# A hybrid decoder block on one core: staggered operand addresses, unit-by-unit mixer pairs and a planned passage

## The chip, the cores and the metric

The kernel runs on one NeuronCore of a Trainium2 chip. The metric is device time in microseconds (us) for one execution; lower is better. The kernel before took 1016.34 us (median of three runs, 1015.45 to 1016.57). TensorE does the matmuls, VectorE (DVE), ScalarE (ACT) and GpSimd (POOL) work on tiles, and transfers are issued on the queues of SyncE (SP) and GpSimd.

## What is computed

One layer on 512 tokens of 1024 channels, in float32: three mixer branches with gates, an output projection, and a convolutional feed-forward part.

```python
h = rmsnorm(x); proj = h @ w_in                 # -> B, C, v | u, ug | q | three gates
y_a = (B * conv3(C * v)) @ w_a_out
y_b = silu(layernorm(conv31(u * sigmoid(ug)) + bias)) @ w_b_out
k, vm = split(rmsnorm(mem) @ w_kv)              # 256 memory tokens, 4 heads
y_c = softmax(q k / 16) vm @ w_att_out
x = x + (sum_i sigmoid(gate_i) * y_i) @ w_o
u = conv3(rmsnorm(x) @ w_up)                    # 2 * 2816 columns
x = x + (silu(u_gate) * u_up) @ w_down
out = rmsnorm(x)
```

## The kernel before

Each float32 operand is split into a high part (rounded to the type that TensorE takes in one pass) and a low part (the rest). A product is three matmuls: high weights by high data, high by low, low by high. A block of weights is a *unit*: 128 x 1024 numbers, loaded by SP into one of six `wf` buffers, copied to `whi` by ACT (L306) and subtracted to `wlo` by DVE (L307). Four pairs of `whi` and `wlo` exist (`UNIT_BUFS`). Splits are written into the program some units ahead of their use.

*Mixer.* Time runs over four heads of keys and values (`k`, `v`), four heads of queries (`q`, `s`, `pt`, `o`), then gated pairs of columns (`ug`, `u`), gates and outputs of three branches (`g`, `y`, `C`, `V`, `B`). Two units hold one pair of 128-wide output columns: unit 0 has the first four blocks of 128 input channels, unit 1 the other four. `next_col` and `project` do one column at a time from both units: 16 matmuls with `whi` (L343, L344), then 8 with `wlo` (L347). Both units are held until the second column is done. Work of other engines is written into the program between columns, by `tick`: jobs that were put `beside` a coming column, and steps of the long convolution.

*Output projection.* `rows_product` computes `row` tiles: four groups of 128 tokens, two halves of 512 columns (L352 to L354). In the second half all matmuls of a token group stand together (24 each), so that each group's sum, norm and transposes (`tr`) can begin before the next group is done.

*Quads.* The matrix w_up is multiplied in a scheme with seven products per block of 2 x 2, the forms 1 to 7, over eleven groups of columns (`QUADS`). A product of form f for group q is `multiply(q, f)`: 24 matmuls of 256 columns (L949). Its moving operand is one of seven pairs of tiles: `fb00`, `fb10` and `fb11` are transposed blocks of the normed rows, and `ft5`, `ft7`, `ft6` and `ft4` are sums of blocks, made in that order, each from the one before. Their fourteen tiles are of 4096 bytes per partition. The weights are sums too: transfers on the POOL queue add to a buffer (L1044) and DVE adds buffers (L1073). ACT and DVE split each unit (L1048, L1052), read the banks back and apply the convolution (L1119, eight steps a group).

*Planner.* From the quads to the end the order is made by `Jobs`: each job has an engine, a cost, the jobs that it follows, and a due time worked out backwards from PE's order; of the jobs that can start first, the one due first is written next. The program order on PE, ACT and DVE is then fixed. Before the planner starts, the passage is written by hand: rows, transposes, `multiply(0, 1)`, splits of the remaining units, transposes of group 2, `multiply(0, 2)`, transposes of group 3. The planner's order goes on with (1,1), (1,2), (0,5), (0,6), (1,5), (0,7), (0,3), (0,4).

*Down.* Seven products with w_down in the same manner (`row` tiles again), then the last norm.

*Addresses.* Pools on the left side of SBUF follow one another after the small constants, pools on the right side hang from the other end. A tile of [128, 1], `mean_col`, stands among the constants on the left. In what follows, the *offset* of a matmul is the address of its moving operand less that of the next matmul's weights, whose load runs beside it, modulo 512 bytes. Offsets by the placement: 256 for the products with `h_hi` and `h_lo`, for keys and values, for all fourteen tiles of the quads and for down (where the units move and `zh`, `zl` are the weights); 448 for `o`, `ya` and the low `yb` tiles as moving operands of `y`, 256 for the high `yb` tiles; 64 for the output projection (the units move, the `mg` tiles are the weights); 192 for the scores `s`; 320 for `o` (`pt` moves, `vh` and `vl` are the weights).

Of the kernel before, what the change touches and what calls it, by code (L numbers as in the profile page):

```python
# [55 lines left out]
LOAD_BUFS = 6  # L56
UNIT_BUFS = 4
# [92 lines left out]
def hybrid_block_kernel(  # L150
# [24 lines left out]
    psum = ctx.enter_context(tc.tile_pool(name="psum", bufs=8, space=bass.MemoryType.PSUM))  # L175

# [146 lines left out]
    pair = {"n": 0}  # L323

    def next_col():

        j = pair["n"] % 2
        pair["n"] += 1
        if j == 0:
            freed[0] = taken[0]  # L330
            taken[0] += 2
            split_to(freed[0] + 3)
            pair["units"] = split[freed[0] : taken[0]]
        else:
            split_to(freed[0] + 4)
        return pair["units"], j

    def project(ps, col, hi, lo):

        (u, j), at = col, slice(col[1] * P, (col[1] + 1) * P)  # L340
        for k in range(KC):
            w_hi = u[k // 4][0][:, k % 4, at]
            nc.tensor.matmul(ps, w_hi, hi(k), start=k == 0, stop=False)  # L343
            nc.tensor.matmul(ps, w_hi, lo(k), start=False, stop=False)  # L344
        for k in range(KC):
            w_lo = u[k // 4][1][:, k % 4, at]
            nc.tensor.matmul(ps, w_lo, hi(k), start=False, stop=k == KC - 1)  # L347
# [64 lines left out]
    mean_col = const.tile([P, 1], F32, tag="mean_col", name="mean_col")  # L412
# [10 lines left out]
    load_to(2)  # L423
    mem_cols = [a_tile("mem") for _ in range(KC // 2)]
    for i, t in enumerate(mem_cols):
        nc.sync.dma_start(
            out=t.rearrange("p (k n) -> p k n", k=2),
            in_=mem_t[i * 2 * P : (i + 1) * 2 * P, :].rearrange("(k p) n -> p k n", p=P),
        )
# [103 lines left out]
    def keep_keys(ps):  # L533
        t = a_tile("k")
        for c in range(2):
            at = (slice(None), slice(c * N_MEM, (c + 1) * N_MEM))
            nc.vector.tensor_tensor(t[at], ps[at], r_mem["row"][:, :N_MEM], op=ALU.mult)
        keys.append(split_tile(t, "k", rows, rows))
# [27 lines left out]
    for h in range(HEADS):  # L566
        ps = p_tile("k")
        for c in range(2):
            project(ps[:, c * N_MEM : (c + 1) * N_MEM], next_col(), m_hi, m_lo)
            if c == 1:  # L570
                beside(2 if h == 0 else 0, lambda ps=ps: keep_keys(ps))
            tick()
# [20 lines left out]
    def queries(h):  # L593
        q = []
        for c in range(2):
            ps = p_tile("q")
            project(ps, next_col(), *hp)
            hi, lo = a_tile("qh", F32R), a_tile("ql", F32R)
            nc.scalar.activation(hi, ps, AF.Copy, scale=Q_SCALE)
            nc.vector.scalar_tensor_tensor(  # L600
                lo, ps, Q_SCALE, hi.bitcast(F32), op0=ALU.mult, op1=ALU.subtract
            )
            q.append((hi, lo))
            if c == 1:
                beside(1, lambda: scores(h, q))
                beside(3, lambda: attend(h))
                beside(4, lambda: weigh(h))
            tick()
# [141 lines left out]
    def glu(m):  # L750
        sg = []
        for _ in range(2):
            ps = p_tile("ug")
            project(ps, next_col(), *hp)
            t = a_tile("sg")
            nc.scalar.activation(t, ps, AF.Sigmoid)
            sg.append(t)
            tick(5)
        for i in range(2):
            ps = p_tile("u")  # L760
            project(ps, next_col(), *hp)
            u = a_tile("u", pool=temp)
            nc.vector.tensor_tensor(u, ps, sg[i], op=ALU.mult)
            u_tiles[m + i] = u
            conv_b_start(m + i)
            tick(4)
# [3 lines left out]
    def short_conv(m):  # L770
        cs, ts = [], []
        for _ in range(2):
            ps = p_tile("C")
            project(ps, next_col(), *hp)
            t = a_tile("C")
            nc.scalar.copy(t, ps)
            cs.append(t)
            tick(5)
        for i in range(2):
            ps = p_tile("V")  # L780
            project(ps, next_col(), *hp)
            nc.vector.tensor_tensor(cs[i], ps, cs[i], op=ALU.mult)
            ts.append(conv3(cs[i], "conv_a_w", m + i, KC))
            tick(2)
        for i in range(2):
            ps = p_tile("B")
            project(ps, next_col(), *hp)
            nc.vector.tensor_tensor(ts[i], ps, ts[i], op=ALU.mult)
            ya.append(split_tile(ts[i], "ya", part, part))
            tick(3)  # L790
# [3 lines left out]
    def gates(b, m):  # L794
        ps = p_tile("g")
        project(ps, next_col(), *hp)
        t = a_tile("g")
        nc.scalar.activation(t, ps, AF.Sigmoid, bias=par("b_gate", b * KC + m))  # L798
        tick(5)
        return t  # L800

    def merge(m, parts, gate, first=False, last=False):
        ps = p_tile("y")
        project(ps, next_col(), lambda k: parts[k][0], lambda k: parts[k][1])
        nc.vector.tensor_tensor(gate, ps, gate, op=ALU.mult)  # L805
        if first:
            merged[m] = gate
        else:
            nc.vector.tensor_tensor(merged[m], merged[m], gate, op=ALU.add)
        if last:  # L810
            merged[m] = split_tile(merged[m], "mg", part, part)
        tick(3)
# [5 lines left out]
    for m in range(0, KC, 2):  # L818
        gate = [gates(2, m + i) for i in range(2)]
        for i in range(2):  # L820
            merge(m + i, o_parts, gate[i], True)
# [3 lines left out]
    for m in range(0, KC, 2):  # L825
        gate = [gates(0, m + i) for i in range(2)]
        for i in range(2):
            merge(m + i, ya, gate[i])
    gate = [gates(1, m) for m in range(KC)]
    assert not conv_todo and not side  # L830
    for m in range(KC):
        merge(m, yb, gate[m], last=True)
# [6 lines left out]
    h2 = h2_pool.__enter__()  # L839

# [4 lines left out]
    def rows_product(half, parts, rows, n_k, staggered, done):  # L845
# [17 lines left out]
        for t in range(NT):  # L863
# [8 lines left out]
            nc.vector.tensor_tensor(rows[t][half], rows[t][half], ps[t], op=ALU.add)  # L872
            if done is not None:
                done(t)
# [7 lines left out]
    def h2_tile(key):  # L882
        return [
            h2.tile([P, 4, HALF], F32R, tag=key + s, name=name("f" + key + s)) for s in "hl"
# [9 lines left out]
    def transpose_rows(xn, t):  # L894
        r, at = t // 2, slice((t % 2) * P, (t % 2 + 1) * P)
        for i in range(2):
            ps = p_tile("tr").rearrange("p (k n) -> p k n", k=4)
            for k in range(4):
                nc.tensor.transpose(ps[:, k, :], xn[i][:, k * P : (k + 1) * P], ident)
            form = h2_forms.get(f"b{i}{r}")  # L900
            if form is not None:
                nc.scalar.copy(form[0][:, :, at], ps)
                nc.vector.tensor_tensor(
                    form[1][:, :, at], ps, form[0][:, :, at].bitcast(F32), op=ALU.subtract
                )
            nc.scalar.copy(blocks[i, r][:, :, at], ps)

    rows_product(0, merged, x1, KC, 0, None)
    h2_n = {}

    def x1_norm(t):
        h2_n[t] = norm_rows(x1[t], g_ffn)
        for i in range(2):
            nc.sync.dma_start(out=x1_kept[t, :, i * 512 : (i + 1) * 512], in_=x1[t][i])
        if 0 < t < NT - 1:
            transpose_rows(h2_n.pop(t - 1), t - 1)

    rows_product(1, merged, x1, KC, KC, x1_norm)
# [35 lines left out]
    for n, f in enumerate(((0, 1), (0, 2), (1, 1))):  # L954
        w_units[f] = split[N_UP + n]
    multiply(0, 1)
    freed[0] = N_UP + 1
    split_to(len(units))
    w_units[1, 2] = split[N_UP + 3]
    transpose_rows(h2_n.pop(2), 2)  # L960
    multiply(0, 2)
    transpose_rows(h2_n.pop(3), 3)

    for p in (part_pool, rows_pool, temp_pool):
        p.__exit__(None, None, None)
    zs = ctx.enter_context(tc.tile_pool(name="zs", bufs=1, side="right", reuse_waits="tile"))
    temps_pool = tc.tile_pool(name="temps", bufs=1, side="right", reuse_waits="tile")
    temps = temps_pool.__enter__()

    jobs = Jobs([("pe", 0, 1), ("pe", 0, 2)], {"DMA": -15.0}, {"wf": LOAD_BUFS})  # L970
# [23 lines left out]

    BLOCK = {"t5": "t5", "t7": (0, 1), "t6": (0, 0), "t4": (1, 0)}
    job("t5", "DVE", dve(1024), sum_t5)
    job("t7", "DVE", dve(1024), sum_t7, ["t5"])
# [16 lines left out]
    order = [(1, 1), (1, 2), (0, 5), (0, 6), (1, 5), (0, 7), (0, 3), (0, 4)]  # L1014
    for q in range(1, QUADS):
        if q > 1:
# [8 lines left out]
    uses = [("pe", q, f) for q, f in order]  # L1025
# [38 lines left out]
    for q in range(QUADS):  # L1064
# [5 lines left out]
        if q > 1:  # L1070
            split_job(("pe", q, 1), (q, 1), src("u"), 4, 256, [("ld", q, "u")])
        split_job(("pe", q, 5), (q, 5), src("s"), 4, 256, [("s5", q)])
# [17 lines left out]
    z = zs.tile([P, 2, PAIRS, SEQ], F32, tag="z", name="z")  # L1090

    def temp2(s, n):
        return temps.tile([P, 2, SEQ], F32, tag=s, name=name(s), bufs=n)
# [31 lines left out]
    def gated(q):  # L1125
        nc.vector.tensor_tensor(z[:, :, q, :], c_t[q, 1], c_t[q, 0], op=ALU.mult)

    for q in range(QUADS):
        pe = lambda f, q=q: ("pe", q, f)
        job(("r1", q), "ACT", actv(512), lambda q=q: read1(q),  # L1130
            [pe(1)] + ([("taps", q - 2, 0)] if q > 1 else []))
# [27 lines left out]
    for q, f in order:  # L1159
        after = []  # L1160
        if (q, f) not in ((1, 1), (1, 2)):
            after.append(("wl", q, f))
        if OPERAND[f][0] == "t":
            after.append(("fl", OPERAND[f]))
# [273 lines left out]
```

## Time and profile before

| | us |
|---|---|
| median of three runs | 1016.34 |
| lowest, highest | 1015.45, 1016.57 |
| time of the profiled execution | 1016.17 |
| its span, first to last instruction | 1014.4 |

The page lists busy time by engine, the span in slices, the chain that ended last, and groups of instructions. "PE" is the matmul, "PEld" the weight load that runs beside it, "PEclk" the granted share of the TensorE clock. The duration of a matmul row includes its passage through the array, so rows overlap: what one matmul costs a stream is the distance from its start to the next start, called the *pitch* here. The page's chain of work merges neighbours, and then shows the pitch as length by count.

### The profile page before, as it was taken

What the parts mean: (1) busy time and instruction counts of PE and PEld (TensorE: products, weight loads), DVE (VectorE), ACT (ScalarE), POOL (GpSimd) and SP (SyncE); (2) the same over time, 40 slices, a digit from 0 to 9 for tenths busy, and PEclk for the clock granted to TensorE, in tenths of its full rate; (3) what the DMA queues carried; (4) which work ended last, traced back from release to release, by engine and by line L of the source; (5) the groups of instructions that cost most, each with busy time, mean ns of one, the idle gap of its engine ahead of it and who ended that gap; (6) DMA issues with size and microseconds to landing.
All of it is one profiled execution on the core that took longest, in us unless ns stands there. A gap on an engine that the chain in (4) does not pass through costs nothing.

```text
span 1014.4 us, 13621 instructions
## 1 busy us (share of the span) xinstructions
PE 986.4 (97%) x5424; PEld 859.1 (85%) x5424; DVE 783.8 (77%) x955; ACT 466.2 (46%) x634; POOL 107.2 (11%) x84
## 2 busy tenths in 40 slices
PE   6999999999999999999999999988999999999997
PEld 6988888888888888888887788878999999988876
DVE  4784548888877888888665365469999999999986
ACT  5554453232222232232255533266767666765556
POOL 3400000000000000000040000102122111101500
PEclk9999999999999999999999999999999999999999
DMA  9642222333323232333232624648887977879972
GB/s 322 191 141 83 63 63 83 91 96 104 99 89 104 83 104 85 103 104 104 88 100 93 197 83 125 163 128 166 188 186 174 201 176 164 179 247 309 270 130 83
DMA packets 122831, 141.10 MB, mean 139 GB/s; under 512 B 4880, under 2 KB 103824, under 8 KB 122768
## 3 DMA queue, kind: packets, MB, share of 16 engines
q1 hardware_dynamic: 100688, 114.28, 35.5%
q0 software_dynamic: 21936, 25.96, 16.0%
q8 instruction: 42, 0.69, 0.3%
q14 instruction: 21, 0.17, 0.1%
q10 hardware_dynamic: 144, 0.01, 0.0%
HBM read 136.03 MB, written 4.19 MB: 138 GB/s over the span
## 4 chain that ended last, share of the span: by engine, by line
PE 90%; DVE 4%; ACT 4%; issue 1%; DMA 1%; POOL 0%; SPq 0%; ACTq 0%; DVEq 0%; POOLq 0%
PE quad L949 20%; PE row L353 5%; PE row L352 5%; PE row L354 5%; PE y L347 4%; PE y L344 4%; PE y L343 4%; PE g L347 4%; PE g L343 4%; PE g L344 4%; PE q L343 1%; PE q L344 1%; PE C L344 1%; PE u L344 1%; PE u L343 1%; PE ug L344 1%
## 5 line engine op out<-in xcount | busy, mean ns | idle before, releaser
L307 DVE TENSOR_TENSOR wlo<-wf,whi 128x1024 fp32r<-128x1024 f32 x123 | 158.8, 1298 | 37.2 <-ACT whi L306 36.4
L680 DVE SCALAR_TENSOR_TENSOR acc<-u,pk,acc 128x511 f32<-128x511 f32 (+14 forms) x240 | 176.7, 738 | 6.1
L306 ACT CAST whi<-wf 128x1024 fp32r<-128x1024 f32 x124 | 128.1, 1045 | 49.4 <-PE y L344 29.4
L1048 ACT CAST whi<-wf 128x1024 fp32r<-128x1024 f32 (+1 forms) x91 | 94.0, 1035 | 59.3 <-PE quad L949 32.3
L1052 DVE TENSOR_TENSOR wlo<-wf,whi 128x1024 fp32r<-128x1024 f32 (+1 forms) x91 | 109.0, 1204 | 10.8 <-ACT whi L1048 10.5
L343 PE MATMUL g<-h_hi,whi 128*128 128x512 f32 x192 | 75.0, 391 | 1.6 <-ACT whi L306 1.6
L1044 POOL DMA_DIRECT2D wf<-in_w_up x33 | 42.5, 1289 | 316.5 <-DVE wlo L1052 126.8
L344 PE MATMUL g<-h_lo,whi 128*128 128x512 f32 x192 | 74.8, 390 | 0.0
L353 PE MATMUL row<-wlo,zh 128*128 128x512 f32 x154 | 60.3, 392 | 1.0 <-DVE wlo L1052 1.0
L352 PE MATMUL row<-whi,zh 128*128 128x512 f32 x154 | 60.1, 390 | 0.1
L354 PE MATMUL row<-whi,zl 128*128 128x512 f32 x154 | 59.9, 389 | 0.0
L798 ACT ACTIVATE g<-g,pk 128x512 f32<-128x512 f32 x24 | 16.5, 689 | 89.8 <-PE g L347 89.7
L347 PE MATMUL g<-h_hi,wlo 128*128 128x512 f32 x192 | 47.4, 389 | 0.0
L805 DVE TENSOR_TENSOR g<-y,g 128x512 f32<-128x512 f32 x24 | 16.6, 692 | 39.8 <-PE y L347 39.8
L343 PEld LDWEIGHTS g<-h_hi,whi 128*128 128x128 f32 x192 | 36.0, 188 | 10.0 <-ACT whi L306 2.4
L344 PEld LDWEIGHTS g<-h_lo,whi 128*128 128x128 f32 x192 | 36.0, 188 | 7.6
L347 PEld LDWEIGHTS g<-h_hi,wlo 128*128 128x128 f32 x192 | 36.0, 188 | 7.5
L688 POOL TENSOR_TENSOR tot<-tot,acc 128x512 f32<-128x512 f32 x6 | 10.6, 1767 | 256.2 <-DVE acc L680 179.4
L353 PEld LDWEIGHTS row<-wlo,zh 128*128 128x128 f32 x154 | 28.9, 188 | 7.8 <-DVE wlo L1052 2.1
L352 PEld LDWEIGHTS row<-whi,zh 128*128 128x128 f32 x154 | 28.9, 188 | 6.7 <-DVE x L1336 0.7
L354 PEld LDWEIGHTS row<-whi,zl 128*128 128x128 f32 x154 | 28.9, 188 | 6.0
L1119 DVE SCALAR_TENSOR_TENSOR c<-u,pk,c 128x511 f32<-128x511 f32 (+1 forms) x44 | 32.2, 747 | 0.6
(273 smaller groups left out, 2818.2 us busy)
## 6 DMA issues: line engine op xcount, KB each, us to landing
wf<-in_w_in SPq DMA_DIRECT2D x72, 512.0 KB, 3.5
wf<-in_w_up SPq DMA_DIRECT2D x46, 512.0 KB, 4.7
wf<-in_w_up POOLq DMA_DIRECT2D x33, 512.0 KB, 6.2
wf<-in_w_kv SPq DMA_DIRECT2D x16, 512.0 KB, 7.0
wf<-in_w_down SPq DMA_DIRECT2D x15, 512.0 KB, 5.8
wf<-in_w_att_out SPq DMA_DIRECT2D x8, 512.0 KB, 3.5
wf<-in_w_a_out SPq DMA_DIRECT2D x8, 512.0 KB, 3.5
wf<-in_w_b_out SPq DMA_DIRECT2D x8, 512.0 KB, 4.8
```

The costliest lines, as they stand in the source:

```text
L306: nc.scalar.copy(hi, src)
L307: engine.tensor_tensor(lo, src, hi.bitcast(F32), op=ALU.subtract)
L343: nc.tensor.matmul(ps, w_hi, hi(k), start=k == 0, stop=False)
L344: nc.tensor.matmul(ps, w_hi, lo(k), start=False, stop=False)
L347: nc.tensor.matmul(ps, w_lo, hi(k), start=False, stop=k == KC - 1)
L352: nc.tensor.matmul(ps, s_hi, w_hi, start=start, stop=False, skip_group_check=again)
L353: nc.tensor.matmul(ps, s_hi, w_lo, start=False, stop=False, skip_group_check=again)
L354: nc.tensor.matmul(ps, s_lo, w_hi, start=False, stop=stop, skip_group_check=again)
L680: nc.vector.scalar_tensor_tensor(acc[:, s:], u_tiles[m][:, : SEQ - s], par("conv_b_w", (K_B - 1 - s) * KC + m), acc[:, s:], op0=ALU.mult, ...
L949: nc.tensor.matmul(ps[:, c, :], w[:, k, at], a[:, k, :], start=first and n == 0, stop=k == 3 and n == 2, skip_group_check=again,)
L1048: nc.scalar.copy(w_units[key][0], src())
L1052: nc.vector.tensor_tensor(lo, src(), hi.bitcast(F32), op=ALU.subtract)
```

## The change

Four things are changed.

1. *Addresses.* `mean_col` moves to a pool `edge` of 224 bytes at the far right end, ahead of the other right-hand pools. A `shift` tile of 32 bytes stands first in the pool of the quads' operands, and each of the fourteen tiles is 32 bytes longer. By the placement, all products `y` and the output projection come to offset 256, as the rest of the mixer's projections; `s` and `o` come to offset 0. The quads' tiles stand at `fb00` 288 and 320 (high, low), `fb10` 352 and 384, `fb11` 416 and 448, `ft5` 480 and 0, `ft7` 32 and 64, `ft6` 96 and 128, `ft4` 160 and 192. Down stays at 256.
2. *Mixer pairs.* `project_pair` takes one unit after the other: per unit both columns, and per block high by high, high by low, low by high. A unit is given back after its own 24 matmuls. `tick` follows each unit, as it followed each column. Two PSUM tiles are open for a pair.
3. *Start.* The two halves of the memory operand that the first unit needs are loaded before the second unit.
4. *Passage.* The second half of the rows does the first unit for all four groups at once (24 matmuls) and then 18 per group. The last group's sum, norm and the transposes of groups 2 and 3, the split of unit (1,2) and the copies of the blocks become jobs of the planner. The order begins (0,1), transposes of group 2, (0,2), (1,1), transposes of group 3, (1,2), (2,1), (2,2), (0,5), and so on. The planner's cost of a quad product goes from 24 x 0.12 to 24 x 0.115.

The matmuls, splits, transfers and bytes are the same in number, except that the keys' sums are read from two tiles.

```diff
+    edge = ctx.enter_context(tc.tile_pool(name="edge", bufs=1, side="right"))
+    mean_col = edge.tile([P, 56], F32, tag="mean_col", name="mean_col")[:, :1]
...
-    def project(ps, col, hi, lo):
-        (u, j), at = col, slice(col[1] * P, (col[1] + 1) * P)
-        for k in range(KC):
-            w_hi = u[k // 4][0][:, k % 4, at]
-            nc.tensor.matmul(ps, w_hi, hi(k), start=k == 0, stop=False)
-            nc.tensor.matmul(ps, w_hi, lo(k), start=False, stop=False)
-        for k in range(KC):
-            w_lo = u[k // 4][1][:, k % 4, at]
-            nc.tensor.matmul(ps, w_lo, hi(k), start=False, stop=k == KC - 1)
+    def project_pair(ps, hi, lo, done, n_conv=0):
+        for g in range(2):
+            w_hi, w_lo = next_unit()
+            for j in range(2):
+                at = slice(j * P, (j + 1) * P)
+                for i in range(4):
+                    k = 4 * g + i
+                    first, last = k == 0, k == KC - 1
+                    nc.tensor.matmul(ps[j], w_hi[:, i, at], hi(k), start=first, stop=False)
+                    nc.tensor.matmul(ps[j], w_hi[:, i, at], lo(k), start=False, stop=False)
+                    nc.tensor.matmul(ps[j], w_lo[:, i, at], hi(k), start=False, stop=last)
+                if g == 1:
+                    done(j)
+            tick(n_conv)
...
-    load_to(2)
     mem_cols = [a_tile("mem") for _ in range(KC // 2)]
     for i, t in enumerate(mem_cols):
+        load_to(1 + i // 2)
...
+    h2.tile([P, SHIFT // 4], F32, tag="shift", name="shift")
...
     def h2_tile(key):
         return [
-            h2.tile([P, 4, HALF], F32R, tag=key + s, name=name("f" + key + s)) for s in "hl"
+            h2.tile([P, 4 * HALF + 8], F32R, tag=key + s, name=name("f" + key + s))[
+                :, : 4 * HALF
+            ].rearrange("p (k n) -> p k n", k=4)
+            for s in "hl"
         ]
...
-    rows_product(1, merged, x1, KC, KC, x1_norm)
+    rows_product(1, merged, x1, KC, KC - 2, x1_done)
...
-    multiply(0, 1)
-    freed[0] = N_UP + 1
-    split_to(len(units))
-    w_units[1, 2] = split[N_UP + 3]
-    transpose_rows(h2_n.pop(2), 2)
-    multiply(0, 2)
-    transpose_rows(h2_n.pop(3), 3)
...
+    t = NT - 1
+    job(("xs", t), "DVE", dve(512), lambda: x1_sum(t, last_row["ps"]), ["wo"])
+    job(("sq", t, 0), "ACT", 1.2, lambda: x1_square(t), [("xs", t)])
+    job(("xn", t), "DVE", 2.3, lambda: x1_scale(t), [("sq", t, 0)], 0.2)
...
-    order = [(1, 1), (1, 2), (0, 5), (0, 6), (1, 5), (0, 7), (0, 3), (0, 4)]
+    order = EARLY + [(2, 1), (2, 2), (0, 5), (0, 6), (1, 5), (0, 7), (0, 3), (0, 4)]
...
+        if (q, f) == (0, 2):
+            job(("tr", 2), "PE", 0.87, lambda: transpose_rows(2))
+        if (q, f) == (1, 2):
+            job(("tr", 3), "PE", 0.87, lambda: transpose_rows(3), [("xn", 3)])
-        job(("pe", q, f), "PE", 24 * 0.12, lambda q=q, f=f: multiply(q, f), after)
+        job(("pe", q, f), "PE", 24 * 0.115, lambda q=q, f=f: multiply(q, f), after)
```

## The prediction

> **What bounds the kernel now.** I read the page first, then busy times by stage, then the chain of waits merged by pitch, then what PE waited for.
>
> ```profile
> span 1014.4 us, 13621 instructions
> ...
> PE 986.4 (97%) x5424; PEld 859.1 (85%) x5424; DVE 783.8 (77%) x955; ACT 466.2 (46%) x634; POOL 107.2 (11%) x84
> ```
>
> PE is the bound, so time can come only from its idle stretches or from a shorter pitch. The busy times by stage (PE's first; after the engines PEclk and the DMA share) say where the 28 us of idle lie and who is next:
>
> ```profile
> 0.00:66.00 66.00, 54.74 (x405) 53.55 (x406) 46.38 (x59) 37.28 (x60) 19.98 (x19) 0.97 0.71 227
> ...
> 440.00:612.00 172.00, 170.41 (x743) 138.88 (x742) 109.87 (x132) 67.82 (x86) 14.68 (x9) 1.00 0.35 110
> 612.00:667.00 55.00, 55.00 (x248) 44.94 (x247) 26.84 (x38) 19.33 (x34) 2.73 (x2) 1.00 0.47 130
> 667.00:702.00 35.00, 28.64 (x219) 27.60 (x218) 29.05 (x31) 23.40 (x33) 6.41 (x5) 0.95 0.69 147
> 702.00:891.00 189.00, 189.00 (x1577) 189.00 (x1577) 177.46 (x198) 125.13 (x155) 33.40 (x26) 1.00 0.84 184
> 891.00:960.00 69.00, 68.33 (x337) 57.93 (x337) 65.62 (x67) 40.12 (x45) 18.65 (x16) 1.00 1.00 285
> ```
>
> The start idles 11.3 us, the passage (667 to 702) 6.4 us with the clock at 0.95. In the quads PE never stops, but DVE (third pair of numbers) is busy 177.5 of 189 us, 94%: it is the next bound. The merged chain gives pitches as length by count:
>
> ```profile
> 188.74 1.81 PE ug L347 x8
> ...
> 237.81 1.87 PE y L347 x8
> ...
> 701.25 190.10 PE quad L949 x1582
> ```
>
> That is 226.7 ns for 512 columns at offset 256, 233.3 at offset 448, and 120.0 for the quads' 256 columns at 256 (120.2 with the gaps of one wait). The half-clock stretches give what streaming alone costs: in 9.84 to 17.3 us the 256 columns of `k` start 213.3 ns apart, so 106.7 at full clock, and 213.3 for 512. Quads and `ug` both pay 13.3 ns over that, `y` pays 20. One stream of 256 columns has another offset, the scores at 192; here are two of its heads, start times in the first column:
>
> ```profile
> 83.56 0.28 PE L352 MATMUL s<-kh,qh 128*128 128x256 f32 x1
> ...
> 84.27 0.28 PE L352 MATMUL s<-kh,qh 128*128 128x256 f32 x1
> ```
> ```profile
> 98.14 0.28 PE L352 MATMUL s<-kh,qh 128*128 128x256 f32 x1
> ...
> 99.16 0.28 PE L352 MATMUL s<-kh,qh 128*128 128x256 f32 x1
> ```
>
> Six matmuls in 0.71 us are 118 ns each, nine in 1.02 us are 113: the same offset settles in two rhythms. The mean over all heads' starts is 114.6. So the pitch does go with where the operands lie. What PE waited for:
>
> ```profile
> PE k L343 <- ACT mh L452: 8.1, 1, 8.1
> PE quad L949 <- DVE ft5l L1007: 2.8, 1, 2.8
> PE g L343 <- ACT whi L306: 1.6, 2, 0.8
> PE quad L949 <- DVE wlo L1052: 1.4, 1, 1.4
> PE quad L949 <- ACT whi L306: 1.4, 1, 1.4
> ...
> PE quad L949 <- DVE wlo L307: 0.8, 1, 0.8
> ```
>
> **The change, part by part.** All sums stand against the profiled execution, 1016.2 us, of which 1014.4 is span; it lies 0.2 under the median of the runs.
>
> *Start: 3 us less.* Half a megabyte (the second unit) no longer goes ahead of the memory operand; at the page's 322 GB/s of the first slice that is 1.6 us. But the third matmul now wants `wlo` of the first unit, which POOL makes from 6.35 to 8.69 us, so PE starts in earnest near 8.5 instead of after its wait for the second `whi` until 11.84. From 8.5, 46 matmuls at 213 ns end near 18.3 (near 16.5 if full clock comes one step sooner); before, they end at 19.2: 0.9 to 2.7 less. Later, PE stands 2 us near 60 us behind a `whi` queued on ACT after `h_hi`, which waits for DVE's `x`; the half clock that follows costs about 1.4 more. Splits now run three units ahead instead of two, but DVE is nearly full from 46 to 70 us, so I take half of that back. Bounds: 0 (DVE eats it all) to 6.
>
> *Gates: 1.9 less.* The two waits of `g` at 554 and 566 us (starts 1.19 apart instead of 0.23) come from units queued on ACT behind the swish of four tiles, 5 us. A unit is now used for 5.4 us and three are ahead: covered. Without that cover the 1.9 us stay.
>
> *Offsets of `y` and of the output projection: 3.8 less.* At 256 like `ug`: 384 matmuls with `o` and `ya` by 6.6 ns are 2.5; 192 with `yb` (now 228.9) by 2.2 are 0.4; 192 of the projection (now about 231.5) by 4.8 are 0.9. Bounds: 0, since `yb` has a rhythm of 229 ns and more even where its offset is 256, and 3.8. `s` and `o` at offset 0 are 144 matmuls; between 113 and 126.7, and 226 and 233, they move 1.2 us at most: counted as nothing.
>
> *Passage: 6 less.* Lost now: 6.4 idle and 5% of 35 us, 1.8, at the lower clock, together 8.1. The chain in the new order, with durations from the rows: the split of (0,1) stands before the rows' norms, so the first quad's two waits (1.4 and 0.8) go. `ft5` needs both last transposes, one copy (0.6), a sum (1.2), ACT's cast (1.05) and DVE's low part (1.2), with three splits of DVE between; products (1,2), (2,1) and (2,2) stand ahead of it, 8.3 us: covered by about 1.5 us, and without it 2.8 and a new half-clock stretch of 1.6 return. What is late next: the first transposes, whose norm now has 4.1 us of matmuls over it instead of 5.6, but takes 4.9 with its table load (649.0 to 653.9): 0.8; and `wlo` of (0,3), last in a row of some seventeen DVE instructions of 1.2 us: about 1.4. So 8.1 less 2.2. The second half's SP writes wait for the sums as before, and the loads queued behind them have their buffers early. Bounds: 2 to 8.
>
> *Quads: 3.5 less.* No row shows thirteen of the fourteen offsets. Bounds by the nearest: 113.3 (a head of `s`) and 126.7 (the 20 ns that `y` pays at 448, put on 106.7). One of the fourteen, `ft4` low, is exactly the 192 of `s`. I take 117, midway between the scores' mean and the present value: 1848 matmuls by 3 are 5.5. Of this DVE takes back some: a quad costs it seven splits of 1.22, eight taps of 0.747, two sums of 0.68, one of 0.69 and two of 1.22, 19.0 us, against 168 x 0.117 = 19.7 of PE, and six instructions of 1.2 for down fall in besides. I charge 2 us. Ends for this term: 12.4 less to 12.4 more.
>
> "TensorE: Matmul & The Clock Gate" of the Trainium skill (Step-by-step) speaks against this part: PE has two independent read ports, and loading the next weights doesn't steal bandwidth from the running matmul. By that no offset would matter. The trace disagrees with 226.7, 233.3, 113 and 118.
>
> Sum: 3 + 1.9 + 3.8 + 6 + 3.5 = 18.2, so 998.
>
> **The rivals.**
>
> *The offsets do nothing* (chance 0.12): the differences of pitch come from rhythm alone, quads stay at 120. For it: one offset has two pitches. Against it: 1600 matmuls in one rhythm without a break. Then only start, gates and passage count, 10.9: 1005.
>
> *DVE becomes the bound* (0.18). From 667 to 960 us it has 272.2 us of work in 293. If it keeps idling 6%, as now in the quads, that stretch can't fall under 289.6. For it: the sums of the passage come in one run. Against it: much of its idling is waiting for `whi`, which waits for PE. Then the last two terms give 3.4 together: 1016.2 - 12.1 = 1004.
>
> *The quads get slower, 122 to 126.7* (0.12): offsets near 0 and 448 are as bad as `y` says; 3.7 to 12.4 lost against 14.7 won: 1005 to 1014.
>
> *The change loses* (0.08): an offset near 0 may cost more than any row shows. It decides from a mean of 120 + 14.7/1.848 = 128 ns on; at 132 it is 1016.2 - 14.7 + 22.2 = 1024.
>
> *Pitch near 113 and DVE keeps up* (0.10): 12.4 for the quads and 16.7 with the full passage: 987.
>
> **How the numbers follow.** The forecast has 0.40, with 993 to 1003 as its own range. From 988 to 1010 about 0.8 lies: the best case, the worst end of slower quads and the losing case are outside. A change of 0.2%, 2 us, is what a measurement here tells from none. Faster by more: all cases but the losing one and the worst end of slower quads, 0.89; within: 0.03; slower: 0.08.
>
> **What would show it.** Quads' matmuls of one form start at their own distance, between 113 and 127 ns, the same for all groups. `y` merges at 1.81 for eight. No wait of PE for `ft5l`; waits for `xn` near the first transposes and for `wlo` of (0,3). DVE over 96% in the quads. I am wrong if the quads' mean lies outside 114 to 121, or if PE waits for DVE more than 6 us between the rows and down.

## The result, and the profile after

The changed kernel takes 1005.84 us (median of four runs, 1003.44 to 1006.45) against 1016.46 for the kernel before (1015.45 to 1016.99): a ratio of 0.9892, 95% interval 0.9874 to 0.991. That is 10.6 us less: inside the range of 988 to 1010, but 7.8 short of the forecast of 998 and outside the 993 to 1003 that the forecast kept as its own. The profiled execution is the fastest of the four (1003.44, granted clock 0.997; the others 0.993 to 0.994), so its span is 12.8 us under that of the kernel before, more than the 10.6 between the medians. Its stages stand like this, in us, each from its first matmul to the next stage's (down is counted from the start of the quads' last matmul):

| | start, to first `q` | `q` to rows | rows | quads | down, to its last matmul |
|---|---|---|---|---|---|
| before | 66.75 | 554.28 | 47.92 | 231.67 | 106.84 |
| after | 62.97 | 549.18 | 45.80 | 223.24 | 113.15 |
| difference | -3.8 | -5.1 | -2.1 | -8.4 | +6.3 |

Four stages gave 19.4 us in this execution, a little more than the 18.2 forecast. Down, which the change doesn't touch, took 6.3 back. The page of the profile after:

```profile
span 1001.6 us, 13638 instructions
...
PE 975.7 (97%) x5424; PEld 853.4 (85%) x5424; DVE 784.7 (78%) x955; ACT 466.4 (47%) x632; POOL 106.5 (11%) x84
```

The busy times by stage (PE's first, DVE's third):

```profile
0.00:66.00 66.00, 55.85 (x420) 54.82 (x421) 48.66 (x59) 37.71 (x61) 20.73 (x19) 0.97 0.71 235
440.00:612.00 172.00, 172.00 (x761) 142.41 (x760) 112.76 (x137) 70.51 (x87) 13.73 (x9) 1.00 0.36 113
612.00:665.00 53.00, 52.94 (x271) 44.76 (x270) 26.82 (x40) 22.29 (x40) 1.44 (x1) 1.00 0.41 118
665.00:700.00 35.00, 33.60 (x283) 33.19 (x282) 33.08 (x34) 24.33 (x33) 10.29 (x8) 1.00 0.96 200
700.00:880.00 180.00, 179.32 (x1514) 178.90 (x1514) 165.22 (x187) 118.73 (x149) 30.84 (x24) 1.00 0.88 187
880.00:950.00 70.00, 63.24 (x279) 50.72 (x278) 67.92 (x69) 39.37 (x44) 20.79 (x18) 1.00 1.06 284
```

The idle time of the gates (440 to 612) is gone, that of the passage (665 to 700) falls from 6.4 to 1.4 at full clock. In the quads DVE is busy 92%, less than the 94% before, and yet in the first 70 us of down PE idles 6.8 us beside a DVE that is busy 97%. What PE waited for:

```profile
PE k L338 <- ACT mh L447: 6.5, 1, 6.5
PE row L348 <- ACT zh L1268: 2.8, 1, 2.8
PE row L348 <- DVE x L1403: 2.4, 2, 1.4
PE ss L469 <- POOL sq L437: 1.9, 1, 1.9
...
PE row L349 <- DVE wlo L1111: 1.3, 2, 0.9
PE quad L990 <- DVE wlo L1111: 1.3, 1, 1.3
```

The waits of `ft5l` and of the gates are gone. New are one for POOL's squares at the start and those of `row` in down. The longest of these, in PE's timeline:

```profile
892.01 0.39 PE L350 MATMUL row<-whi,zl 128*128 128x512 f32 x1
895.21 0.50 PE L348 MATMUL row<-whi,zh 128*128 128x512 f32 x1 [2.81 <-ACT zh L1268]
```

ACT casts that `zh` from the last product z (L1186), and DVE's timeline shows where the z was:

```profile
880.98 1.22 DVE L1186 TENSOR_TENSOR z<-c,c 128x1024 f32<-128x1024 f32 x1
...
884.38 2.98 DVE L1179 SCALAR_TENSOR_TENSOR c<-g,pk,c 128x511 f32<-128x511 f32 x4
...
888.41 2.98 DVE L1179 SCALAR_TENSOR_TENSOR c<-u,pk,c 128x511 f32<-128x511 f32 x4
891.49 1.23 DVE L1186 TENSOR_TENSOR z<-c,c 128x1024 f32<-128x1024 f32 x1
```

The quads' last matmul starts at 881.19. DVE still has the z of group 9 in hand and ends that of group 10 at 892.7, 11.5 us after the quads. Before, this lag was 7.9 us. So DVE came late out of a stage in which it had idled 8%.

### The profile page after: what moved, and what is told of

The parts are those of the page before. It is cut to its first block, busy times and chain, and to the rows that moved or that the text cites. A ratio compares the mean times of both kernels' runs of the same rounds, so it can differ in the third digit from the quotient of the medians.

```text
span 1001.6 us, 13638 instructions
## 1 busy us (share of the span) xinstructions
PE 975.7 (97%) x5424; PEld 853.4 (85%) x5424; DVE 784.7 (78%) x955; ACT 466.4 (47%) x632; POOL 106.5 (11%) x84
## 5 line engine op out<-in xcount | busy, mean ns | idle before, releaser
L311 ACT CAST whi<-wf 128x1024 fp32r<-128x1024 f32 x123 | 128.3, 1048 | 182.7 <-issue 74.6
L312 DVE TENSOR_TENSOR wlo<-wf,whi 128x1024 fp32r<-128x1024 f32 x122 | 154.4, 1271 | 57.0 <-ACT whi L311 56.3
L676 DVE SCALAR_TENSOR_TENSOR acc<-u,pk,acc 128x511 f32<-128x511 f32 (+14 forms) x240 | 181.3, 758 | 6.1
L1107 ACT CAST whi<-wf 128x1024 fp32r<-128x1024 f32 x92 | 93.8, 1036 | 60.3 <-PE quad L990 38.0
L1111 DVE TENSOR_TENSOR wlo<-wf,whi 128x1024 fp32r<-128x1024 f32 x92 | 108.9, 1204 | 12.3 <-ACT whi L1107 11.7
L340 PE MATMUL g<-h_hi,wlo 128*128 128x512 f32 x192 | 74.7, 389 | 0.0
L794 ACT ACTIVATE g<-g,pk 128x512 f32<-128x512 f32 x24 | 16.5, 690 | 37.0 <-PE g L340 37.0
L1179 DVE SCALAR_TENSOR_TENSOR c<-g,pk,c 128x511 f32<-128x511 f32 (+1 forms) x44 | 32.4, 747 | 0.5
```

What stands on the lines that cost most here:

```text
L311: nc.scalar.copy(hi, src)
L312: engine.tensor_tensor(lo, src, hi.bitcast(F32), op=ALU.subtract)
L340: nc.tensor.matmul(ps[j], w_lo[:, i, at], hi(k), start=False, stop=last)
L676: nc.vector.scalar_tensor_tensor(acc[:, s:], u_tiles[m][:, : SEQ - s], par("conv_b_w", (K_B - 1 - s) * KC + m), acc[:, s:], op0=ALU.mult, ...
L1107: nc.scalar.copy(w_units[key][0], src())
L1111: nc.vector.tensor_tensor(lo, src(), hi.bitcast(F32), op=ALU.subtract)
```

## The experiments

Three theories for down: D, VectorE's work in quads and down takes the same time whatever PE does; P, the planner's cheaper quad product (24 x 0.115 for 24 x 0.12) makes an order in which work for down is left behind the quads; and S, which came out of the first answers, told below. Stage times are those of each run's profiled execution.

| run | start | quads | down | median | 95% interval of the ratio to before |
|---|---|---|---|---|---|
| the change | 62.97 | 223.24 | 113.15 | 1005.84 | 0.9874 to 0.991 |
| addresses alone | 65.30 | 229.72 | 106.78 | 1009.55 | 0.9912 to 0.9945 |
| change, quads at 256 | 61.50 | 225.66 | 117.29 | 1008.07 | 0.9902 to 0.9935 |
| change, cost 0.12 | 60.93 | 221.30 | 107.31 | 994.03 | 0.9765 to 0.9794 |
| change, four jobs early | 63.15 | 222.25 | 113.78 | 1002.98 | 0.9847 to 0.9877 |
| change, cost 0.125 | 62.98 | 230.65 | 106.79 | 1002.36 | 0.9823 to 0.9878 |
| cost 0.12, quads at 256 | 64.42 | 224.47 | 107.19 | 998.42 | 0.9803 to 0.9836 |
| cost 0.12, quads at 448 | 62.66 | 220.31 | 107.55 | 991.29 | 0.9719 to 0.9775 |
| change, VectorE's costs | 62.96 | 228.44 | 107.70 | 1001.78 | 0.9836 to 0.9885 |
| all together | 59.04 | 228.66 | 106.60 | 998.30 | 0.9807 to 0.984 |
| 0.12, 448, norm later | 59.05 | 220.04 | 107.33 | 987.53 | 0.9699 to 0.9726 |

**Addresses alone.** The kernel before, with `edge`, `shift` and the eight more words of each tile.

> The kernel before with the new addresses alone (mean_col at the far end, 32-byte steps of the fourteen tiles). Forecast's reading: y and the output projection save 3.8 us and the quads about 3.4 (pitch 118 in the place of 120): 7.2 less than before, near 1009. Theory D (VectorE's work from the first quad to about 949 us takes 291 us whatever PE does, so what the quads gain is given back in down): the quads get about 3 us shorter, down as much longer, and only the mixer's part is left: 3 to 4.5 less, near 1012.5.

Measured: 7.1 less than before (1009.55 against 1016.66). Quads 1.9 shorter (the pitch of 118.2 is worth 3.3, of which 1.6 went into a second stretch of half clock behind the passage's waits, 0.89 over 15 us), down unchanged at 106.8. Nothing is given back: theory D falls in its simple form, and the forecast's reading of the addresses holds.

**The change with the quads at 256.**

```diff
-    h2.tile([P, SHIFT // 4], F32, tag="shift", name="shift")
...
-            h2.tile([P, 4 * HALF + 8], F32R, tag=key + s, name=name("f" + key + s))[
-                :, : 4 * HALF
-            ].rearrange("p (k n) -> p k n", k=4)
-            for s in "hl"
+            h2.tile([P, 4, HALF], F32R, tag=key + s, name=name("f" + key + s)) for s in "hl"
```

> The changed kernel with all fourteen tiles of the quads at offset 256 again, everything else kept. If the quads' gain counts: pitch 120.0, quads 3 to 4 us longer, down still 113, so 3.4 above the changed kernel. Theory D: quads longer by 3 to 4, down shorter by as much (109 to 110), total within 1 us of the changed kernel.

The median is 2.2 above the change, for 3.4 expected, with intervals that overlap. Pitch 120.0 again, quads 2.4 longer. Down didn't get shorter, as D wanted, but 4.1 longer, with the same waits as after the change (2.8 for `zh`, 2.4 for `x`). What is added is the clock: 0.91 over 880 to 900, which holds the wait for `zh`, and behind two waits near 950 (0.9 us for a `wlo`, then 1.4 for `x`) this stretch, PEclk third from the end:

```profile
950.00:960.00 10.00, 8.56 (x26) 6.52 (x25) 8.30 (x9) 3.77 (x4) 0.06 (x1) 0.66 1.13 206
```

At 0.66 some 3.4 us are lost in these ten, and 1.8 in the others. The same waits stand in the change's profile at full clock; that its slower executions (up to 1006.45) fell to half clock there too is likely by their lower granted clock, but they have no profile.

**The cost alone.** `24 * 0.115` back to `24 * 0.12`, one number.

> The changed kernel with the planner's cost of a quad product put back from 24 x 0.115 to 24 x 0.12. Theory P (the 6.3 us that down got longer come from the order that the cheaper cost makes: jobs for down wait behind work of the quads): down falls back to 107 to 109, total 4 to 6 below the changed kernel. Theory D: order hardly matters, quad start to last matmul stays at 336 within 1.5 us.

994.03, 11.8 us less than the change, where P had 4 to 6. Quads 1.9 and down 5.8 shorter; another 2.0 of the profile lie in the start, where the two programs are the same. Theory P's place is right (down was to be 107 to 109, and is 107.31). The number acts through the planner's clock, not through its due times: with 0.12 in the due times alone the program comes out as with 0.115, instruction for instruction, and with 0.12 in the clock alone as with 0.12. PE's order is the same in both; 250 places of DVE's order and 169 of ACT's differ. DVE around the end of the quads (877.26) with 0.12:

```profile
874.07 1.22 DVE L1186 TENSOR_TENSOR z<-c,c 128x1024 f32<-128x1024 f32 x1
...
877.53 2.98 DVE L1179 SCALAR_TENSOR_TENSOR c<-g,pk,c 128x511 f32<-128x511 f32 x4
...
881.56 2.98 DVE L1179 SCALAR_TENSOR_TENSOR c<-u,pk,c 128x511 f32<-128x511 f32 x4
884.65 1.23 DVE L1186 TENSOR_TENSOR z<-c,c 128x1024 f32<-128x1024 f32 x1
```

The z of group 9 is done before the quads end, the taps of group 10 follow at once. And yet this order does more before the last z. Four instructions of 1.22 us (difference and sum of z's first two pieces, L1250 and L1033) stand inside the quads with 0.12, as in the kernel before, and behind them with 0.115.

**Four jobs early.** The change with 0.115, and these four tied to the products z of groups 8 and 9:

```diff
-        job(("z", q), "DVE", dve(1024), lambda q=q: gated(q), [("silu", q), ("taps", q, 1)])
+        early = {QUADS - 3: [("zs", "c", 0)], QUADS - 2: [("zs", "c", 1)]}.get(q, [])
+        job(("z", q), "DVE", dve(1024), lambda q=q: gated(q),
+            [("silu", q), ("taps", q, 1)] + early)
```

> The changed kernel with its cost of 24 x 0.115, and one constraint for the planner: the difference and the sum of the first piece of z (zd 0, zs c 0) come before the product z of group 8, those of the second piece (zd 1, zs c 1) before that of group 9, as the kernel before and the one with cost 0.12 have them. Theory P (the cheaper cost makes the planner see VectorE full, so it leaves these four instructions, 4.9 us, behind the quads, where VectorE has no idle time; in the quads it has 8%): down falls from 113 to 107 to 109, the time from 1005.8 to 995 to 1000. Rival: the order of the quads themselves (ScalarE's splits, waits inside the quads) is what the 0.115 spoils: then down stays at 112 or more, the time at 1003 or more.

A miss, and the rival's case: down stays at 113.78, and the median is 2.9 lower with intervals that overlap. The last z only came later, 16.8 us after the quads' last matmul. The four are a symptom. So where does DVE lose its time? Its stretch from the first quad to the last z, and its longest entry among the waits in it, for the change:

```profile
658.00:892.70 234.70, 232.31 (x1913) 229.23 (x1911) 215.75 (x242) 158.42 (x204) 41.13 (x32) 1.00 0.88 194
```
```profile
DVE wlo L1111 <- ACT whi L1107: 11.7, 24, 1.5
```

and for cost 0.12:

```profile
656.00:885.90 229.90, 229.22 (x1903) 227.43 (x1902) 219.80 (x246) 158.03 (x203) 41.12 (x32) 1.00 0.88 193
```
```profile
DVE wlo L1111 <- ACT whi L1107: 4.1, 12, 1.1
```

DVE idles 19.0 us in the one (234.7 less 215.75) and 10.1 in the other, which has the four instructions more (246 against 242). Most of the difference (7.6 of 8.9) is waits of low parts for high parts. From this comes theory S, a reading that the next runs test: a group costs the planner some 19.0 us of DVE, and of PE 168 x 0.115 = 19.3 (20.2 with 0.12). It takes DVE for nearly full, so it keeps no work in hand and writes each `wlo` close behind its `whi`; on the chip PE is slower (118 ns) and DVE quicker (1.13 us from one instruction of 1024 to the next, for 1.22 planned), the high parts wait for PE to give buffers back (38.0 us of ACT's waits, 26.1 with 0.12), and DVE, which keeps to the written order, waits with them. By S, that is why it comes out of the quads late.

**VectorE's costs.** 0.115 kept, DVE's costs from the trace:

```diff
-        return (n + 151) / 960.0
+        return (n + 64) / 960.0
...
-                    job(keys[-1], "DVE", dve(560), lambda a=(q, value, i, s): conv_tap(*a),
+                    job(keys[-1], "DVE", dve(630), lambda a=(q, value, i, s): conv_tap(*a),
```

> The changed kernel with its cost of 24 x 0.115, but the planner's costs of VectorE put to the distances of the traces: 1.13 us in the place of 1.22 for 1024 elements, 0.723 in the place of 0.741 for a tap. Theory S (what counts is the planner's clock: at 0.115 against 1.22 it takes VectorE for full and writes its order so that low parts stand right behind the high parts they wait for; on the chip VectorE then idles 19 us up to the last z, 10 with the cost 0.12): VectorE's idle time from the first quad to the last z falls to 8 to 13 us, quads plus down from 336.4 to 327 to 331, the time to 992 to 999. Rival (a PE cost below the real pitch is itself the fault, whatever VectorE's costs): quads plus down stay at 334 or more, the time above 1002.

By the numbers set beforehand S fails here: DVE's idle time is 16.5, not 8 to 13, quads plus down are 336.1, not 327 to 331, and the time is 1001.78. The rival's 334 or more came in, and its 1002 was missed by 0.2. But the two stages differ. Down falls to 107.70 with the 0.115 in place, and the last z is 7.9 us behind the quads: for down it is the two costs against each other that matter, and a PE cost below the real pitch doesn't lengthen it by itself. The quads are 5.2 longer than the change's: PE lost 6.6 us at 797 to 806 behind one `whi` that waited 6.3 for its transfer, the half clock after it included.

**Cost 0.125 and all together.** `24 * 0.125`; and, in the second, 0.118, costs of DVE and ACT from the traces, 0.15 us of delay on high parts, all tiles at 448, and the norm of `x` one step later:

```diff
-    beside(8, x_scale)
-    beside(9, x_scale_rows)
+    beside(9, x_scale)
+    beside(10, x_scale_rows)
```

> The changed kernel with the planner's cost at 24 x 0.125, above the 0.118 measured. Theory P: what matters is that VectorE looks less than full to the planner; the four instructions stay in the quads, time within 2 us of that with 0.12 (992 to 996). Rival: 0.12 was a lucky order, and any other cost gives another time: outside 990 to 998.

> The changed kernel with all planner costs from the traces (quad product 24 x 0.118, VectorE as in the run with its costs alone, ScalarE 62 ns less an instruction, a high part usable 0.15 us late), all fourteen tiles at offset 448, and the norm of x one step later, so that PE doesn't wait 1.9 us for POOL's squares at 37.7 us. Theory S and the streams: start 2 us shorter and without its occasional half clock (first q at 59 to 61), quads plus down 325 to 329, time 985 to 990. If the order is luck: quads plus down above 331, time above 992.

Both times lie where the rivals had them (1002.36, 998.30). Both orders cure down (106.79, 106.60), and both lose some 7 us at once in the quads, more with the half clock behind it. ACT in the run with everything together, and PE's wait:

```profile
764.37 1.06 ACT L1212 ACTIVATE c<-c 128x1024 f32<-128x1024 f32 x1 [2.11 <-DVE c L1176]
774.18 1.04 ACT L1104 CAST whi<-wf 128x1024 fp32r<-128x1024 f32 x1 [8.75 <-DMA wf<-in_w_up]
```
```profile
PE quad L987 <- ACT g L1193: 7.3, 2, 6.6
```

ACT stands 8.75 us at the head of its order for one late transfer; behind it waits the copy of a bank that PE needs. Less that wait and the half clock behind it (8.4 of 228.66), these quads are 220.3, as with 0.12 at 448. So the rival is right on the quads: each of these three orders has its own late transfer, that of 0.12 happens to have none, and costs nearer to the chip's don't avoid them. What made the transfers late wasn't tried. The start, by contrast, did as expected: 59.04.

On down, S's numbers fit once DVE's one long wait in the runs with VectorE's costs, with 0.125 and with everything together is set aside: it then idles 10.6 to 11.3 us, for 10.1 with 0.12 and 18.9 in the change. But S's reason doesn't hold. The planner gives each job a start time, and these times, from the kernels of the runs, say how far behind the quads the last z is planned to end; beside them is what was measured from the start of the quads' last matmul:

| order | planned, us | measured, us |
|---|---|---|
| the kernel before | 7.8 | 7.9 |
| the change | 12.0 | 11.5 |
| change, four jobs early | 17.0 | 16.8 |
| change, cost 0.12 | 8.8 | 8.6 |
| change, cost 0.125 | 7.6 | 7.9 |
| change, VectorE's costs | 7.6 | 7.9 |
| all together | 7.5 | 7.9 |

The lag is in the plan, where DVE hardly waits (2.8 us up to the change's last z): the written order sets it, and DVE's waits on the chip add nothing to it. Nor does a full DVE mark the bad order: planned, it is busy 99% of the quads in the change, with 0.12 and in the kernel before. Why the planner puts the last z late with one pair of costs and not with another stays open.

**Quads at 256 and at 448 with cost 0.12.** The first is the change without `shift` and the longer tiles, the second has `SHIFT = 192` and tiles of 4096 bytes.

> The changed kernel with cost 24 x 0.12 and all fourteen tiles of the quads at offset 256. If PE sets the end here: pitch 120.0 in the place of 118.2, so 1848 x 1.8 ns = 3.3 us more than 994.0, 996 to 998. If VectorE sets it (theory D): within 1 us of 994.0.

> The changed kernel with cost 24 x 0.12 and all fourteen tiles of the quads at one offset, 448, where the streams ran in two rhythms, 117.8 and 113.4. If the fast rhythm holds: quads' pitch near 113.4 and up to 8.9 us of matmul time less; VectorE, 92% busy at 118, then decides: 988 to 993. If the slow rhythm holds: pitch 117.8, time within 1.5 us of 994.0. By the forecast's reading of y (448 is bad, 126.7): 15 us more, 1009.

At 256 the median is 4.4 above cost 0.12, and the quads 3.2 longer (pitch 120.0 for 118.2): with an order that has neither fault PE sets the time, and the offsets count in full. The longest piece of the merged chain, cost 0.12 and then the same with the quads at 256:

```profile
666.38 201.74 PE quad L990 x1704
```
```profile
669.97 204.66 PE quad L986 x1704
```

At 448 the matmuls ran at 117.8 for most of the quads and at 113 in 41% of the last group, after a short wait. The median is 2.7 lower, but the four runs spread from 987.28 to 994.20.

**Streams.** Matmuls alone.

> No layer is computed: only streams of matmuls in the quads' pattern (high by high, high by low, low by high), 72 of 256 columns for each of the sixteen offsets in steps of 32 bytes, then 24 of 512 columns each, then 72 of 256 columns again with VectorE and ScalarE busy beside them; high and low tile at the same offset. The forecast's reading (pitch is a function of the offset): a table between 113 and 127, worst near 448 and 0, the same with and without company. Rival R (rhythm: one offset has several pitches, company or the switching decides): pitches of one offset differ between the two passes or within one stream, and show no order by offset. Rival C (contention with other engines' accesses makes the extra 7 to 13 ns): near 107 quiet, 113 to 120 with company.

Mean pitch in ns of the streams of 256 columns, by offset; two values are two rhythms:

```
offset mod 256   0      32           64             96     128    160          192            224
                 120.0  116.7-117.8  117.8 / 113.3  120.0  118.7  117.3-118.7  117.8 / 113.4  118.3
```

Offsets 256 apart behave alike, and DVE and ACT at work beside change nothing in kind: contention (C) falls. Neither of the other two readings holds whole: there is an order by offset, against R, but 448 isn't the worst, and 320 and 448 had 117.8 in the first pass and 113.4 in the second, as R said. With 512 columns, offsets 0 and 256 have 227 to 228, 64 and 320 have 228.9, all others 233 to 234. In the streams only the moving operand's address changes. That the weights' address counts too shows in the kernel before: in the output projection and in down the same unit buffers move, but ten starts take 2.33 us in the one (from 639.87, weights `mg`, offset 64) and eight take 1.81 in the other (from 949.73, weights `zh` and `zl`, offset 256), pitches of 233 and 226. The projection's 233 is not the 228.9 of the streams at 64, so the table doesn't cover every stream.

**Rhythm after waits.**

> No layer is computed: streams of 48 matmuls of 256 columns in the quads' pattern, eight for each of the offsets 64, 192, 320, 448, 160 and 256, each stream after a short wait of PE for a VectorE copy of its bank (32 to 256 columns long); then streams that pass from one offset to another without a wait. Reading W (a wait draws the rhythm anew, and it then holds): at 64, 192, 320 and 448 each stream runs wholly at 117.8 or wholly at 113.3, both occurring; 256 always 120. Reading F (fixed by the offset before): streams after waits of one offset all have one pitch, and 480 to 448 and 352 to 320 always give 113.3.

The merged chain (start, length, what) shows three streams at offset 64 and one at 256, each after a short wait:

```profile
61.27 5.94 PE bank L136 x48
...
67.64 5.72 PE bank L136 x48
...
73.84 5.94 PE bank L136 x48
```
```profile
286.04 6.02 PE bank L136 x48
```

The lengths include the first matmuls after the wait and the passage of the last. Once settled, the starts lie 117.8 ns apart in the pieces of 5.94 us, 113.3 in that of 5.72 and 120.0 at offset 256. At 64, 192, 320 and 448, 14 of 32 streams ran at 113.3 and 18 at 117.8, each in one rhythm once it had settled; 256 always had 120. W holds: a wait (0.28 to 0.52 us here) draws the rhythm, and it stays. Offset 160 had 117.3 in seven streams and 118.8 in one. Without a wait, passing to one of these offsets from another gave 113.3 in 16 of 18 cases.

**0.12, 448, norm later.** The order without a late transfer, with the two gains that don't touch it.

> The changed kernel with cost 24 x 0.12 (the order that has no long wait in the quads), all fourteen tiles at offset 448, and the norm of x one step later (which took the start to 59.0 us in the run with everything together). If the parts add: start near 59, quads near 220, down near 107.5: 2 to 4 us under the 991.3 of cost 0.12 with 448, so 987 to 989. If the start's gain is lost behind the next wait: 991.

987.53 (986.00 to 990.25), ratio 0.9713 (0.9699 to 0.9726): the parts add, and it beats both kernels. In the profiled execution nine products of the quads ran at 113.3, from 687 us until a stall of 0.28 us at 712; the others ran at 117.8.

## Why the prediction was right, and where it was wrong

Start, gates and passage are read from the trace of the whole change; no run takes one of them alone.

*Start, 3 less:* 3.8 in the profile. The waits near 60 are gone, and PE starts in earnest at 8.8, for 8.5 forecast. The size is in part a draw: eight runs have the same program up to `q` and reach it between 60.93 and 64.42. Missed was the wait for POOL's squares, 1.9 us near 38, and what can follow it. Two executions with the same program to this point, cost 0.12 with the quads at 256 and then cost 0.12 (PEclk third from the end):

```profile
38.00:42.00 4.00, 2.23 (x12) 2.23 (x13) 2.98 (x5) 0.73 (x2) 1.72 (x1) 0.78 0.74 233
42.00:46.00 4.00, 4.00 (x21) 4.00 (x20) 1.65 (x2) 0.46 (x1) 0.00 (x0) 0.50 0.66 210
```
```profile
38.00:42.00 4.00, 2.63 (x22) 2.63 (x23) 2.88 (x6) 1.20 (x2) 1.32 (x1) 1.00 0.73 215
42.00:46.00 4.00, 4.00 (x36) 4.00 (x35) 2.88 (x5) 1.57 (x2) 0.00 (x0) 1.00 0.75 247
```

The first falls to half clock and reaches `q` at 64.42, the second doesn't and is there at 60.93. With the norm one step later the wait is gone, and `q` starts at 59.05.

*Gates and merges, 1.9 and 2.9:* right. The gates' waits are gone, all `y` run at 226.7 (before 233.3 and 228.9), `q` to rows is 5.1 shorter for 4.8 forecast.

*Passage, 6:* right. The losses left were forecast as 0.8 and 1.4; the trace has 0.4 at the first transposes and 1.9 at product (0,3). `ft5l` is covered. PE's waits for VectorE from the rows to the end of the quads are 1.3 us, far below the 6 named as a refutation.

*Quads, 5.5 for the offsets:* the mechanism right, the size off. The pitch is 118.2, not 117, so 1848 x 1.8 = 3.3 us. The value was taken midway towards the scores' 114.6, as if a pitch belonged to an offset; the scores' 113 is the quick one of two rhythms that a wait draws. The scores, moved to offset 0, went to 119.6. And 126.7 as the upper bound came from `y` at 448, which is a bad offset for 512 columns and not for 256. Each form at its own distance was hardly so: 117.8 to 118.8.

*"DVE takes back 2":* the step that failed. VectorE took back 6.3 in down, and 1.9 more in the quads, by the step from cost 0.12. The cause is an edit of the change that the prediction didn't price, 0.115 for 0.12. It reads like a mere estimate, but the order of ACT and DVE is written from it. The sign that the prediction gave for a full VectorE, over 96% in the quads, was looked for in the wrong place: it was 92% there and 97% in down. With 0.12 kept, the sum comes out at 22.6 less (994.03 against 1016.66), 4.4 more than forecast. The rival "DVE becomes the bound" (1004) came near the time by luck: it let DVE keep idling 6% as if that were a property of the work, and it is one of the order. In the order of 0.12 DVE idles 4% of its stretch, in that of 0.115 8%, and what costs the time is where that order puts the last z.

## What to carry to other kernels

Where a planner writes the order, its cost figures are code: compare the orders they make, per engine, before calling such an edit free, and read off the planner's own time for the work that the next stage waits for: here it gave the lag of the last z within 0.5 us. An engine that is busy 92% and idles in waits for its neighbours' latest output hasn't got 8% in hand; see which order makes it wait, and look for the price one stage later. Where a matmul stream's pitch varies, take the offset between moving tile and next weights as a candidate, and a single pitch seen at one offset as one draw.

## What the runs showed of the hardware

The pitch of 256-column matmuls goes with the offset modulo 256 bytes, 113.3 to 120.0 (streams), and at 64 modulo 128 has two stable values, 113.3 and 117.8, that a wait of 0.28 to 0.52 us can switch. By the Trainium skill, "TensorE: Matmul & The Clock Gate" (Step-by-step), loading the next weights takes no read bandwidth from the running matmul. Read so, no offset should count; the streams, with nothing else at work, disagree with 113.3 to 120.0.

The half clock came after PE waits of 0.9 and 1.4 us, 1.4 us apart (near 950, quads at 256), of 2.8 us (near 895, the same run) and of 1.9 us (near 38, in six of the eight executions with that start); the same waits passed at full clock in other executions. The same page of the Trainium skill (Part 1: The HAM clock gate) puts the fall after an idle window of about 3.4 us; these waits were shorter, and the measurement decides.
